# Two encoder layers on one core: the borders of the stages laid out anew, and the first stage ordered by hand

## The chip, the cores and the metric

The kernel runs on one core of one Trainium2 chip. The time is device microseconds of one execution; lower is better. A core has TensorE (PE, matmuls; its weight loads are listed as PEld), VectorE (DVE), ScalarE (ACT), GpSimd (POOL) and SyncE (SP, which here issues every DMA). SBUF is the working memory, PSUM the eight banks that matmuls write. Each engine takes its instructions in a fixed order, the one in which the program was laid out.

## The reference, cut to what matters

512 tokens of width 1024 pass through two layers. `c` gives six rows (shift, scale, gate, twice) per layer.

```
c_act = silu(c)
for l in range(2):
    mod = c_act @ w_mod[l] + b_mod[l]
    sh1, sc1, gt1, sh2, sc2, gt2 = split(mod, 6)
    h = rms_norm(x, g_norm_mix[l]) * (1 + sc1) + sh1
    q_d, k_d, v_d, cq, ckv, k_rope = split(h @ w_in[l])
    o_dil = dilated_attention(rms_norm(q_d), rms_norm(k_d), v_d, positions)   # 8 heads of 64
    o_mla = latent_attention(cq, ckv, k_rope, positions, ...)                 # 8 heads, low-rank q and kv, rotary part
    x = x + gt1 * (concat[o_dil, o_mla] @ w_out[l])
    h = rms_norm(x, g_norm_mlp[l]) * (1 + sc2) + sh2
    x = x + gt2 * (square(relu(h @ w_mlp_in[l])) @ w_mlp_out[l])
```

## The kernel before

x is kept transposed: eight tiles `xT[j]` of 128 features by 512 tokens. Every matmul operand is split into a high and a low part, and each product is three matmuls (`mm3`, L237: lines L238, L239, L240): high by high, low by high, high by low. A weight tile is loaded into a `raw` buffer by a DMA, its high part made by ACT (L233) and its low part by POOL (L234), into buffers named `wh` and `wl`, four each (`load_split`, L229).

The order of work on each engine is not the program's. A planner simulates the program with estimated costs and gives each engine its next ready instruction, the earliest in the program first; that order is then fixed. Three things bind it: `tc.manual_schedule(engines=...)` keeps the instructions of a block on the named engines in the program's order among themselves, `keep_in_program_order` pins one instruction behind what its engine has been given before, and `issue_after` queues what follows on an engine behind one instruction. Buffers are shared by tag: a tile waits until one of the tag's buffers is free (`BUFS`, L61). PSUM has four banks `mm`, two `sc` and two `tr`.

The stages, layer by layer:

- **Setup (L86 to L154, L188 to L196).** Load c, x and small tables; silu of c, spread over the 128 partitions by two matmuls with a matrix of ones (L117) and copied to the SBUF tile `cb` (L118); the squares of x are summed (L121 to L128); the angles of the rotary part are made on POOL and their sines on ACT (L133 to L151), with one load of ACT's function table before and one after.
- **First stage of layer 0 (L694 to L753).** Sixteen rows of w_mod (512 KB each) are loaded and multiplied with `cb` on DVE, which also sums them (`mod_block`, L162). From the sum over x comes 1/rms (`inv_rms`, L244). For each k of eight feature groups: u = x/rms on DVE, high part of h and the full value on ACT (L732, L733), low part alternately on POOL (L735) and DVE (L723), then matmuls with two groups of weights: PR0 (columns of the first pair of dilated heads: q, k, v, 384 columns) and W (the latent columns: cq, ckv and the rotary key, 416 columns), for all four blocks of 128 tokens, which takes all eight PSUM banks. Only DVE is ordered by hand here. After the last k come the chains: the norms of q and k (`chain`, L428; `rsqrt_tiny`, L218), the same for W (L504), the transposes (`tail`, L453 and L521), the rotary tables (`rope_tables`, L484) and the distances for the bias (`distances`, L304).
- **First stage of layer 1 (L755 to L759).** The same weights, PR0 for the four token blocks, then W; norms of the two token halves come from the end of the MLP before (L883).
- **Attention (L761 to L788).** Eight stages of two heads, `st` 0 to 3 dilated, 4 to 7 latent. While the heads of one stage run, `weave` puts in the projection of the next (PR1, PR2, ...), weight loads, the remaining rows of w_mod and, from stage 4, the output projection of the dilated half (`out_dil`). The due times are the numbers of `TUNE`. A head (L327) takes four query blocks: scores, softmax, four transposes into a `tr` bank (L358), the high and low part of the transposed weights (L361, L362), and at the end the product with the values (L368) and the output (L371, L641, L642).
- **Projection 2 (L790 to L812).** The output projection of the latent half, for each half of 256 tokens: eight output tiles, each a sum over four head pairs; the fourth needs the last stage's output. In the first half up to three tiles have their first three products made before a fourth product is asked for. Then `norm` (L277) for that half.
- **MLP (L839 to L883).** Groups of 8, 8, 8, 4 and 4 blocks of 128 hidden features, each with its part of the second matrix. The first four blocks run by token halves, all others over 512 tokens. In layer 0 two rows of w_mod are taken at each other block (`next_mod`, L855).

Of the kernel before, what the change touches and what calls it, by code (L numbers as in the profile page):

```python
# [16 lines left out]
L = 2  # L17
# [20 lines left out]
    MV5=(6.55,), MP0=(3.45,), MP1=(8.6,), W0=(13.54,), W1=(21.5,), W2=(33,),  # L38
# [4 lines left out]
def trunk(ctx: ExitStack, tc: tile.TileContext, a):  # L43
# [28 lines left out]

    def ps(tag, shape=(128, 512)):
        return psum.tile(list(shape), F32, tag=tag, bufs=BUFS[tag], name=nm(tag))
# [15 lines left out]
    cols = [col(N_COL, f"cols{l}") for l in range(L)]  # L90
    SY.dma_start(cols[0], a["cols"][0])
    posc = const.tile([128, 4], I32, name="posc")
    SY.dma_start(posc, a["pos"].rearrange("(t p) -> p t", p=128))
    inv = col(16, "inv")
    SY.dma_start(inv, bass.AP(tensor=a["inv"].tensor, offset=a["inv"].offset, ap=[[0, 128], [1, 16]]))

    xT = [const.tile([128, S], F32, name=f"x{j}") for j in range(8)]
    for j in range(8):
        SY.dma_start(xT[j], a["xT"][j])
    ones = const.tile([128, 128], F32, name="ones")  # L100
# [3 lines left out]


# [5 lines left out]
    cb = const.tile([128, D], F32, name="cb")  # L111
    for i in range(2):
        p = ps("sc", (128, 4, 128))
        dg = s2([128, 4, 128])
        for k in range(4):
            V.tensor_scalar(dg[:, k], ident, cs[:, 4 * i + k:4 * i + k + 1], None, op0=OP.mult)
        T.matmul(p.rearrange("p k c -> p (k c)"), ones, dg.rearrange("p k c -> p (k c)"), start=True, stop=True)  # L117
        A.activation(cb[:, 512 * i:512 * i + 512], p.rearrange("p k c -> p (k c)"), AF.Copy)  # L118


    sq0 = s2(tag="o")  # L121
    for j in range(8):
        if j == 0:
            A.activation(sq0, xT[j], AF.Square)
        else:
            sq = s2(tag="P")
            A.activation(sq, xT[j], AF.Square)
            V.tensor_tensor(sq0, sq0, sq, op=OP.add)  # L128


    pf = col(4, "pf")
    V.tensor_copy(pf, posc)
    ang, kf, w_ = s2([128, 4, 16]), s2([128, 4, 16]), s2([128, 4, 16], tag="b")  # L133
    for t in range(4):
        G.tensor_scalar(ang[:, t], inv, pf[:, t:t + 1], 0.0, op0=OP.mult, op1=OP.add)
    G.tensor_scalar(kf, ang, 1.0 / (2 * math.pi), 12582912.0, op0=OP.mult, op1=OP.add)
    G.tensor_scalar(kf, kf, -12582912.0, 0.0, op0=OP.add, op1=OP.add)
    c1 = 6.28125
    c2 = float(np.float32(np.round((2 * math.pi - c1) * 2.0 ** 20) / 2.0 ** 20))
    c3 = 2 * math.pi - c1 - c2  # L140
    for cc in (c1, c2, c3):
        G.tensor_scalar(w_, kf, -cc, 0.0, op0=OP.mult, op1=OP.add)
        G.tensor_tensor(ang, ang, w_, op=OP.add)
    PI_ = 3.1415925
    G.tensor_scalar(ang, ang, PI_, -PI_, op0=OP.min, op1=OP.max)
    A.activation(kf, ang, AF.Abs)
    G.tensor_scalar(kf, kf, -1.0, math.pi / 2, op0=OP.mult, op1=OP.add)
    sin = const.tile([128, 4, 16], F32, name="sin")
    cos = const.tile([128, 4, 16], F32, name="cos")
    A.activation(sin, ang, AF.Sin)  # L150
    A.activation(cos, kf, AF.Sin)  # L151
    pre = A.preload_act_table_set("natural_log_exp_and_others")
    tc.keep_in_program_order(pre)
    ctx.enter_context(tc.issue_after(pre.ins))  # L154
# [7 lines left out]
    def mod_block(l, i, tag="raw", pool_=False, pin=False, out=None):  # L162
        out = modc[l][:, i:i + 1] if out is None else out
        w = t4(tag, [128, D], F32)
        SY.dma_start(w, a["wmod"][l, i])
        if pool_:
            G.tensor_tensor(w, w, cb, op=OP.mult)  # L167
            A.activation(w, w, AF.Copy, accum_out=out)
        else:
            r = V.scalar_tensor_tensor(w, w, 1.0, cb, op0=OP.mult, op1=OP.mult, accum_out=out)  # L170
            if pin:
                tc.keep_in_program_order(r)
# [19 lines left out]
    def first_norm(j):  # L192

        A.activation(modc[0][:, j:j + 1], mraw[:, j:j + 1], AF.Identity, bias=cols[0][:, C_BMOD + j:C_BMOD + j + 1])
        A.activation(amix[0][:, j:j + 1], mraw[:, 8 + j:9 + j], AF.Identity, bias=gb0[:, j:j + 1],
                     scale=cols[0][:, C_GMIX + j:C_GMIX + j + 1])  # L196

# [31 lines left out]
    def load_split(src, n, raw="raw"):  # L229
        raw = t4(raw, [128, 1024], F32)[:, :n]  # L230
        hi, lo = t4("wh", [128, 1024])[:, :n], t4("wl", [128, 1024])[:, :n]
        SY.dma_start(raw, src)
        A.activation(hi, raw, AF.Copy)  # L233
        G.tensor_tensor(lo, raw, f(hi), op=OP.subtract)  # L234
        return hi, lo
# [8 lines left out]
    def inv_rms(p, v, y, t):  # L244

        V.tensor_scalar(v, p, 1.0 / D, EPS, op0=OP.mult, op1=OP.add)
        A.activation(t, v, AF.Ln)
# [3 lines left out]
        V.scalar_tensor_tensor(y, t, 1.5, p, op0=OP.add, op1=OP.mult)  # L251
# [52 lines left out]
    def distances():  # L304

        posr = s2([128, S], I32)
        SY.dma_start(posr, bass.AP(tensor=a["pos"].tensor, offset=a["pos"].offset, ap=[[0, 128], [1, S]]))
# [10 lines left out]
        dist = [t4("ot", [128, 2, S], F32) for _ in range(2)]  # L318
        for qb in range(4):
# [3 lines left out]
        g = t4("ot", [128, 896], F32)  # L323
        SY.dma_start(g, a["lnc"])
        return dist, g
# [52 lines left out]
    for l in range(L):  # L378
# [19 lines left out]
        def group(src, n):  # L398
            ws = {}

            def load(i, raw="raw"):
                hi, lo = load_split(src[i], 2 * n, raw)
                ws[i] = (hi.rearrange("p (k n) -> p k n", k=2), lo.rearrange("p (k n) -> p k n", k=2))

# [4 lines left out]
            return [lambda i=i, **kw: load(i, **kw) for i in range(4)], step  # L409

        def blocks(w, n, step, chain):
            for tb in range(4):
                st = {}

                def mm(k, tb=tb, st=st):
                    if k == 0:
                        st["b"] = ps("mm")
# [5 lines left out]
        def dil_prep(pr, k_outer=False):  # L423
            w = dict(mm=[], chain=[])
            w["load"], step = group(a["win"][l, pr], 384)
            R = {}

            def chain(tb, bank):  # L428
# [4 lines left out]
                if t == 0:  # L433
                    R[half] = t4("pt" if k_outer else "zz", [128, 2, 4, 2, 64], F32)
                    R["sq"], R["bank"] = s2([128, 8, 64]), bank
                sq = R["sq"]
                A.activation(sq[:, 4 * t:4 * t + 4].rearrange("p h d -> p (h d)"), bank[:, 0:256], AF.Square, scale=1.0 / 8)
                src = bank[:, 256:384].rearrange("p (h d) -> p h d", h=2)
                vt = R["VD"][:, tb]
                A.activation(vt[:, :, 0], src, AF.Copy)  # L440
                V.tensor_tensor(vt[:, :, 1], src, f(vt[:, :, 0]), op=OP.subtract)
                if t == 0:
                    return

                v = small(8)
                V.tensor_reduce(v, sq, axis=AX.X, op=OP.add)
                rs = rsqrt_tiny(v, 8, bank)
                for u, bk in enumerate((R["bank"], bank)):
                    src = bk[:, 0:256].rearrange("p (h o d) -> p h o d", h=4, o=1).to_broadcast([128, 4, 2, 64])
# [496 lines left out]
```

## Time and profile before

| | |
|---|---|
| median of 3 runs | 1368.05 us (1367.66 to 1368.26) |
| the profiled execution | 1368.62 us |
| its span in the profile | 1366.8 us |
| mean granted clock of TensorE | 0.975 |
| bytes moved | 167.59 MB |
| rows of w_mod multiplied in the MLP of layer 0 (L170, `pt`) | 56, 1804 ns each |

The profile is of one execution. Its rows count an engine's busy time; idle time before an instruction is put down to what released it. A row of the table by stretch gives start and end, the length, the busy time of each engine with its number of instructions, the mean clock that was granted to TensorE, the share of the DMA engines that were busy, and GB/s. A row of the timeline gives the start, the length, the engine, the line, the operation, the tiles and, in brackets, the idle time before it and what ended it.

### The profile page before, as it was taken

How to read it: one execution, taken by the hardware profiler on the slowest of the kernel's cores; microseconds unless marked ns; L12 is line 12 of the kernel's file. 1: busy time of each engine (PE TensorE's matmuls, PEld its weight loads, DVE VectorE, ACT ScalarE, POOL GpSimd, SP SyncE). 2: the span in 40 equal slices, each digit the busy share in tenths (PEclk: the TensorE clock that was granted, in tenths of full speed). 3: DMA queues.
4: the chain of work that ended last, by engine and by line, in shares of the span. 5: the costliest groups of instructions: out<-in, count | busy, mean ns of one | idle time of the engine just before them, and what ended most of it. 6: DMA issues, size and time to landing. Idle time of an engine off the chain costs nothing.

```text
span 1366.8 us, 19167 instructions
## 1 busy us (share of the span) xinstructions
PE 1275.1 (93%) x6922; PEld 1109.2 (81%) x6922; DVE 752.4 (55%) x1588; ACT 673.9 (49%) x1389; POOL 651.0 (48%) x504
## 2 busy tenths in 40 slices
PE   3879979898899999999998999999889999999999
PEld 2878867787888888888898988788688888888888
DVE  6677888876661752825574566987662122121223
ACT  5567888875532332322344766887654133232321
POOL 5636785571554444444443533454145444444441
PEclk7989999999999999999999999999999999999999
DMA  9325552331163663845522433211013223223321
GB/s 344 111 95 170 181 164 90 118 124 63 63 224 115 218 229 103 294 142 188 170 82 63 132 124 111 74 45 62 1 63 108 93 93 108 93 93 100 101 93 62
DMA packets 57247, 167.59 MB, mean 123 GB/s; under 512 B 8641, under 2 KB 10817, under 8 KB 57153
## 3 DMA queue, kind: packets, MB, share of 16 engines
q1 hardware_dynamic: 57152, 166.38, 37.0%
q8 instruction: 54, 0.88, 0.3%
q14 instruction: 41, 0.33, 0.1%
HBM read 155.87 MB, written 10.49 MB: 122 GB/s over the span
## 4 chain that ended last, share of the span: by engine, by line
PE 72%; DVE 6%; ACT 5%; issue 4%; POOL 4%; DMA 3%; POOLq 0%; DVEq 0%; ACTq 0%
PE mm L238 21%; PE mm L239 21%; PE mm L240 21%; PE tr L368 3%; PE tr L358 2%; POOL wl L234 2%; DMA raw<-in_wout_dram 1%; DVE pt L362 1%; ACT wh L233 1%; DVE P L343 1%; POOL raw L167 1%; PE sc L238 1%; PE mm L459 1%; PE sc L239 1%; PE sc L240 1%
## 5 line engine op out<-in xcount | busy, mean ns | idle before, releaser
L234 POOL TENSOR_TENSOR wl<-raw,wh 128x1024 fp32r<-128x1024 f32 (+3 forms) x188 | 425.4, 2266 | 449.6 <-ACT wh L233 431.4
L233 ACT ACTIVATE wh<-raw 128x1024 fp32r<-128x1024 f32 (+3 forms) x188 | 189.0, 1005 | 273.7 <-PE mm L240 206.4
L649 DVE SCALAR_TENSOR_TENSOR x<-mm,mod,x 128x512 f32<-128x512 f32 (+1 forms) x144 | 89.1, 629 | 259.9 <-PE mm L240 259.5
L238 PE MATMUL mm<-h,wh 128*128 128x512 f32 (+1 forms) x608 | 224.5, 370 | 7.1 <-ACT h L274 7.1
L239 PE MATMUL mm<-h,wl 128*128 128x512 f32 (+1 forms) x608 | 224.6, 370 | 0.0
L240 PE MATMUL mm<-h,wh 128*128 128x512 f32 (+1 forms) x608 | 221.7, 369 | 1.1 <-POOL h L271 1.1
L238 PE MATMUL mm<-ot,wh 128*128 128x512 f32 (+1 forms) x448 | 154.1, 347 | 4.9 <-ACT ot L641 4.1
L239 PE MATMUL mm<-ot,wl 128*128 128x512 f32 (+1 forms) x448 | 153.1, 344 | 0.0
L240 PE MATMUL mm<-ot,wh 128*128 128x512 f32 (+1 forms) x448 | 150.7, 346 | 0.6 <-POOL ot L642 0.6
L822 ACT ACTIVATE P<-mm 128x512 f32<-128x512 f32 (+1 forms) x72 | 39.2, 551 | 203.9 <-PE mm L240 203.9
L238 PEld LDWEIGHTS mm<-h,wh 128*128 128x128 f32 x608 | 116.2, 191 | 26.1 <-ACT h L274 7.5
L239 PEld LDWEIGHTS mm<-h,wl 128*128 128x128 f32 x608 | 116.1, 191 | 19.0 <-POOL wl L234 0.3
L240 PEld LDWEIGHTS mm<-h,wh 128*128 128x128 f32 x608 | 114.5, 190 | 20.3 <-POOL h L271 1.6
L823 DVE SCALAR_TENSOR_TENSOR mm<-mm,P 128x512 f32<-128x512 f32 (+1 forms) x72 | 45.4, 636 | 138.6 <-ACT P L822 138.6
L238 PE MATMUL mm<-wh,h 128*128 128x384 f32 (+1 forms) x288 | 98.7, 357 | 15.8 <-ACT h L732 9.8
L239 PE MATMUL mm<-wh,h 128*128 128x384 f32 (+1 forms) x288 | 101.8, 354 | 5.1 <-POOL h L735 3.6
L238 PE MATMUL mm<-qk,wh 128*128 128x512 f32 (+1 forms) x288 | 105.3, 366 | 1.0 <-DVE x L649 1.0
L239 PE MATMUL mm<-qk,wl 128*128 128x512 f32 (+1 forms) x288 | 105.2, 365 | 0.0
L240 PE MATMUL mm<-qk,wh 128*128 128x512 f32 (+1 forms) x288 | 105.2, 365 | 0.0
L355 POOL TENSOR_SCALAR P<-P,hs 128x512 f32<-128x512 f32 x64 | 48.4, 756 | 116.5 <-DVE hs L348 94.8
L240 PE MATMUL mm<-wl,h 128*128 128x384 f32 (+1 forms) x288 | 100.2, 351 | 0.0
L170 DVE SCALAR_TENSOR_TENSOR pt<-pt,cb 128x1024 f32<-128x1024 f32 x56 | 99.1, 1804 | 0.0
(248 smaller groups left out, 2667.1 us busy)
## 6 DMA issues: line engine op xcount, KB each, us to landing
raw<-in_w_dram SPq DMA_DIRECT2D x64, 512.0 KB, 3.3
pt<-in_wmod_dram SPq DMA_DIRECT2D x56, 512.0 KB, 4.8
raw<-in_w2a_dram SPq DMA_DIRECT2D x48, 512.0 KB, 3.4
raw<-in_wmod_dram SPq DMA_DIRECT2D x24, 512.0 KB, 3.6
raw<-in_win_dram SPq DMA_DIRECT2D x30, 384.0 KB, 3.2
bias<-b SPq DMA_DIRECT2D x32, 256.0 KB, 2.1
raw<-in_wout_dram SPq DMA_DIRECT2D x16, 512.0 KB, 3.4
raw<-in_w2b_dram SPq DMA_DIRECT2D x16, 512.0 KB, 3.3
```

Of the source, the lines that this page charges most:

```text
L170: r = V.scalar_tensor_tensor(w, w, 1.0, cb, op0=OP.mult, op1=OP.mult, accum_out=out)
L233: A.activation(hi, raw, AF.Copy)
L234: G.tensor_tensor(lo, raw, f(hi), op=OP.subtract)
L238: T.matmul(out, sh, mh, start=first, stop=False)
L239: T.matmul(out, sl, mh, start=False, stop=False)
L240: T.matmul(out, sh, ml, start=False, stop=last)
L355: G.tensor_scalar(P, P, r_, 0.0, op0=OP.mult, op1=OP.add)
L358: T.transpose(tr[:, kc], P[:, kc * 128:(kc + 1) * 128], ident)
L368: T.matmul(po[:, HALF[qh]], vals(hd, kc), pt[qh][w][:, kc], start=(kc == 0 and w == 0), stop=(kc == 3 and w == 1))
L649: V.scalar_tensor_tensor(xT[j][:, hf], p, gt[:, j:j + 1], xT[j][:, hf], op0=OP.mult, op1=OP.add)
L822: A.activation(r, p, AF.Relu)
L823: V.scalar_tensor_tensor(p, p, 0.0, r, op0=OP.max, op1=OP.mult)
```

## The change

It has six parts; the lines are of the diff below.

1. **silu's row in PSUM.** The two `tr` banks become one tile `trp`, used in turns by every later user of the tag. In the first stage it holds silu's row (`cbp`), which DVE reads directly; the copy to `cb` is made at the stage's end.
2. **The first stage by hand.** SP, DVE, ACT and POOL are all in the program's order. x is loaded before the small tables. The exponential's table is loaded at the start; the sines move to the end of the stage (`rotary`, on DVE), with the two table loads behind them. Two of the squares go to POOL; 1/rms goes to PSUM; every low part of h goes to POOL. The rows of w_mod are loaded ahead into `qk` buffers, weights are loaded and split at fixed places. In the loop over k only PR0's four token blocks and W's first are multiplied; W's other blocks come after the loop, the second in an `sc` bank, the third and fourth in `mm` banks that PR0's chain sets free. The distances are made at the end of the loop; the rotary tables move to stage 1.
3. **Projection 2.** In the first half, tiles 4 to 7 get their first three products and a first addition to x, tiles 0 to 3 get them and are held in their banks; the fourth products come last. The second half stays as it was. The last weight tile of it is split into `zz` buffers.
4. **The MLP's first eight blocks** run by token halves (four before). Their weight tiles are split into `pt`, `qk` and `wh`/`wl` buffers. In layer 0 the eight rows of w_mod of that group come during the second half.
5. **Layer 1's first stage**: PR0 blocks 0 and 1, W blocks 0 and 1, then PR0 2 and 3, W 2 and 3. W's weights are loaded at once, into `ot` and `pt` buffers; PR0's blocks 2 and 3 use `sc` banks; PR0's norms are made for each block instead of for each pair.
6. `TUNE`: W1 from 21.5 to 29.5.

```diff
+    trp = psum.tile([128, 2, 512], F32, name="trp")
+    turn = [0]
     def ps(tag, shape=(128, 512)):
+        if tag == "tr":
+            turn[0] ^= 1
+            v = trp[:, turn[0]]
+            return v.rearrange("p (a b) -> p a b", a=shape[1]) if len(shape) == 3 else v
...
+    def exp_tables():
+        pre = A.preload_act_table_set("natural_log_exp_and_others")
+        tc.keep_in_program_order(pre)
+        ctx.enter_context(tc.issue_after(pre.ins))
...
-        A.activation(cb[:, 512 * i:512 * i + 512], p.rearrange("p k c -> p (k c)"), AF.Copy)
...
+    def rotary():
...
+        A.activation(sines, sines, AF.Sin)
+        exp_tables()
...
-    def inv_rms(p, v, y, t):
+    def inv_rms(p, v, t):
+        A.activation(t, p, AF.Ln, bias=epsc, scale=1.0 / D)
         V.tensor_scalar(v, p, 1.0 / D, EPS, op0=OP.mult, op1=OP.add)
-        A.activation(t, v, AF.Ln)
...
+            with tc.manual_schedule(engines={E.SP, E.DVE, E.Activation, E.Pool}):
+                for k in range(8):
+                    mods(k)
+                    if k % 2 == 0:
+                        weights(k // 2)
...
+                A.activation(sqp, xT[0], AF.Square)
+                for j in range(1, 8):
+                    sq = s2(tag="P")
+                    if j in (1, 4):
+                        G.tensor_tensor(sq, xT[j], xT[j], op=OP.mult)
+                    else:
+                        A.activation(sq, xT[j], AF.Square)
+                    V.tensor_tensor(sq0 if j == 7 else sqp, sqp, sq, op=OP.add)
+                T.matmul(p, ones, sq0, start=True, stop=True)
...
+                splits(0)
+                mod_mul(8)
+                mod_mul(0)
+                inv_rms(p, v, t)
+                for k in range(8):
...
+                    V.tensor_tensor(u, xT[k], p, op=OP.mult)
+                    first_norm(k)
+                    A.activation(hi, u, AF.Identity, bias=be, scale=ga)
+                    A.activation(u, u, AF.Identity, bias=be, scale=ga)
+                    G.tensor_tensor(lo, u, f(hi), op=OP.subtract)
+                    if k % 2 == 0 and k < 6:
+                        splits(k // 2 + 1)
+                    if k < 7:
+                        mod_mul(9 + k)
+                        mod_mul(k + 1)
+                    for tb in range(4):
+                        PR[0]["step"](banks[tb][:, :384], k, tb)
+                    W["step"](lbanks[0][:, :W_C], k, 0)
+                gains()
+                dist = distances(posr)
+                for i in range(2):
+                    A.activation(cb[:, 512 * i:512 * i + 512], cbp[:, 512 * i:512 * i + 512], AF.Copy)
+            lbanks.append(ps("sc"))
+            for k in range(8):
+                W["step"](lbanks[1][:, :W_C], k, 1)
...
+            for fn in PR[1]["load"][:2]:
+                fn(keep=True)
             for tb in range(4):
                 PR[0]["do_chain"](tb, banks[tb])
+            for tb in (2, 3):
+                lbanks.append(ps("mm"))
+                for k in range(8):
+                    W["step"](lbanks[tb][:, :W_C], k, tb)
...
+            for n, (w, tb) in enumerate(((PR[0], 0), (PR[0], 1), (W, 0), (W, 1), (PR[0], 2), (PR[0], 3), (W, 2), (W, 3))):
+                ev += spread(w["mm"][tb], 4 * n, 4 * n + 3.6) + [(4 * n + 3.8, w["chain"][tb])]
...
+            if l == 0 and st == 1:
+                ev += [(2, W["rope"])]
...
+        hf, held = HALF[0], {}
+        for j in (4, 5, 6, 7, 0, 1, 2, 3):
+            p = ps("mm")[:, :256]
+            out_lat(j, p, hf, (0, 1, 2), True, j >= 4)
+            if j >= 4:
+                add_x(j, hf, p, gt1)
+            else:
+                held[j] = p
+        for j in range(8):
+            p = held[j] if j < 4 else ps("mm")[:, :256]
+            out_lat(j, p, hf, (3,), j >= 4, True)
+            add_x(j, hf, p, gt1)
+        norm(hf, amlp[l], modc[l][:, 24:32], h2h, h2l)
...
+            tags = ("wh", "wl") if i >= 4 else ("pt", "pt") if i < 2 else ("qk", "qk")
...
+            ws = [w1_tile(i) for i in range(8)] if grp[0] == 0 else []
...
                 for hf in HALF:
-                    for i in range(4):
+                    for i in range(8):
                         mlp1(i, hf, ws[i])
+                        if l == 0 and hf.start and i:
+                            next_mod(tag="pt", pin=True)
+                            if i == 7:
+                                next_mod(tag="pt", pin=True)
```

More of the change, by code (lines that the diff above doesn't have):

```diff
@@ L99, in trunk @@
         SY.dma_start(xT[j], a["xT"][j])
+    cols = [col(N_COL, f"cols{l}") for l in range(L)]
+    SY.dma_start(cols[0], a["cols"][0])
     ones = const.tile([128, 128], F32, name="ones")
@@ L146, in trunk @@
[L146 to L154, printed above, removed]
+        T.matmul(cbp[:, 512 * i:512 * i + 512], ones, dg.rearrange("p k c -> p (k c)"), start=True, stop=True)
@@ L407, in step, with blocks @@
                     ws[k // 2][0][:, k % 2], ws[k // 2][1][:, k % 2], k == 0, k == 7)
-            return [lambda i=i, **kw: load(i, **kw) for i in range(4)], step
-        def blocks(w, n, step, chain):
+            return [lambda i=i, **kw: load(i, **kw) for i in range(4)], step, put
+        def blocks(w, n, step, chain, tags=("mm",) * 4):
             for tb in range(4):
@@ L424, in dil_prep @@
             w = dict(mm=[], chain=[])
-            w["load"], step = group(a["win"][l, pr], 384)
+            w["load"], step, w["put"] = group(a["win"][l, pr], 384)
             R = {}
@@ L441, in chain @@
[L441 to L449, printed above, removed]
-                    scl = rs[:, 4 * u:4 * u + 4].rearrange("p (h o d) -> p h o d", o=1, d=1).to_broadcast([128, 4, 2, 64])
-                    V.tensor_tensor(R[half][:, u], src, scl, op=OP.mult)
+                    R[half] = t4("pt" if pr == 0 else "zz", [128, 2, 4, 2, 64], F32)
@@ new lines, in chain @@
+                if nb == 2:
+                    values()
+                if len(got) == nb:
+                    v = small(4 * nb)
+                    V.tensor_reduce(v, sq, axis=AX.X, op=OP.add)
+                    rs = rsqrt_tiny(v, 4 * nb, bank)
+                    for u, (t_, bk) in enumerate(got):
+                        src = bk[:, 0:256].rearrange("p (h o d) -> p h o d", h=4, o=1).to_broadcast([128, 4, 2, 64])
+                        scl = rs[:, 4 * u:4 * u + 4].rearrange("p (h o d) -> p h o d", o=1, d=1).to_broadcast([128, 4, 2, 64])
+                        V.tensor_tensor(R[half][:, t_], src, scl, op=OP.mult)
@@ L479, in dil_prep @@
             else:
-                blocks(w, 384, step, chain)
+                blocks(w, 384, step, chain, ("mm", "mm", "sc", "sc") if pr == 0 else ("mm",) * 4)
             return w
@@ L501, in latent @@
             w = dict(mm=[], chain=[])
-            w["load"], step = group(a["winc"][l], W_C)
+            w["load"], step, w["put"] = group(a["winc"][l], W_C)
             def chain(tb, bank):
@@ L741, in trunk, with mods, weights, splits @@
-            gains()
+            ml, wr = {}, {}
+            def mods(k):
+                ml[8 + k] = mod_load(0, 8 + k, "qk")
+                ml[k] = mod_load(0, k, "qk")
+            def weights(i):
+                raw = ("raw", "zz")[i % 2]
+                wr[i] = load(a["win"][0, 0, i], 768, raw), load(a["winc"][0, i], 2 * W_C, raw)
+            def splits(i):
+                PR[0]["put"](i, *split(wr[i][0], 768))
+                W["put"](i, *split(wr[i][1], 2 * W_C, ("ot", "ot") if i < 2 else ("wh", "wl")))
@@ L745, in trunk @@
+            for fn in PR[0]["tail"]:
                 fn()
```

234 lines of the change are left out of this document (106 added, 128 removed).

## The prediction

> **What bounds the kernel now.** I read the page's head first, then the busy time by stretch of the span, then the waits of TensorE (PE), and last the timeline at each border.
>
> ```profile
> span 1366.8 us, 19167 instructions
> PE 1275.1 (93%) x6922; PEld 1109.2 (81%) x6922; DVE 752.4 (55%) x1588; ACT 673.9 (49%) x1389; POOL 651.0 (48%) x504
> ```
>
> PE is the bound: 1275.1 of 1366.8 us, so 91.7 us of idle time is all that an edit without fewer matmuls can win, plus what the matmuls lose at a low granted clock. The table by stretch says where the idle time lies (first number: length; second: PE busy; PEclk is the mean granted clock).
>
> ```profile
> core 0: us, PE busy (x) PEld busy (x) DVE busy (x) ACT busy (x) POOL busy (x), PEclk, DMA share, GB/s
> 0.00:25.50 25.50, 5.86 (x6) 1.68 (x6) 14.70 (x43) 14.26 (x24) 11.62 (x20) 0.74 0.89 323
> 45.00:70.30 25.30, 21.78 (x104) 19.63 (x102) 14.57 (x27) 14.73 (x30) 18.25 (x18) 0.93 0.13 35
> 70.30:80.30 10.00, 4.94 (x21) 3.88 (x22) 8.62 (x25) 7.52 (x35) 3.30 (x2) 0.83 0.42 139
> 116.00:315.00 199.00, 180.10 (x1115) 157.59 (x1113) 159.47 (x387) 158.23 (x371) 133.03 (x137) 0.97 0.41 132
> 315.00:332.00 17.00, 12.80 (x88) 10.82 (x88) 9.21 (x19) 10.07 (x21) 4.65 (x5) 1.00 0.23 79
> 350.40:376.00 25.60, 21.49 (x161) 20.87 (x161) 15.85 (x42) 14.15 (x34) 13.57 (x19) 0.93 0.17 55
> 709.60:735.00 25.40, 20.78 (x105) 19.09 (x104) 15.71 (x40) 14.32 (x32) 15.84 (x20) 0.87 0.25 71
> 965.00:987.00 22.00, 16.88 (x116) 14.29 (x115) 12.78 (x26) 14.74 (x31) 4.74 (x6) 1.00 0.01 1
> 1005.60:1031.00 25.40, 21.30 (x160) 20.69 (x159) 16.04 (x42) 13.86 (x33) 13.66 (x18) 0.93 0.16 57
> ```
>
> Length less busy time: 19.6 + 3.5 + 5.1 us in the first stage's rows, 4.2 and 5.1 at the two last heads (315 and 965), 4.1 and 4.1 where the MLP begins (350 and 1005), 4.6 where layer 1 begins (709). The waits give the names:
>
> ```profile
> PE mm L238 <- ACT h L274: 11.1, 3, 4.1
> PE mm L238 <- ACT h L732: 9.8, 2, 9.5
> PE mm L238 <- ACT ot L641: 4.1, 2, 2.1
> PE mm L459 <- ACT mm L223: 3.0, 1, 3.0
> ```
>
> The 11.1 us are three waits for the first h of the second token half (two MLPs, one layer start); 9.8 is the first h of the program; 4.1 is the last head's output, once per layer; 3.0 the first chain. The change puts other matmuls in front of each of these.
>
> **First stage, the start.** Before, it runs so:
>
> ```profile
> 13.98 2.08 PE L713 MATMUL sc<-o,ones 128*128 128x512 f32 x2 [5.41 <-DVE o L128]
> 15.60 1.28 ACT L150 ACT_TABLE_LOAD   x1
> 19.82 0.61 ACT L247 ACTIVATE b<-b 128x512 f32<-128x512 f32 x1
> 21.79 0.69 DVE L249 TENSOR_TENSOR b<-b,sc 128x512 f32<-128x512 f32 x1 [4.81 <-ACT sc L248]
> 23.95 0.69 DVE L728 TENSOR_TENSOR pt<-x,P 128x512 f32<-128x512 f32 x1
> 25.55 1.65 PE L238 MATMUL mm<-wh,h 128*128 128x384 f32 x4 [9.48 <-ACT h L732]
> ```
>
> The sum of squares is ready at 16.06, but the logarithm (L247) starts at 19.82, behind the sine table, the second load and a split. The change moves sines and both loads out, drops two copies of silu's row, gives two squares to POOL and issues x before three small transfers. I put the sum at 13.9 (about 2 us earlier, an estimate); the logarithm now stands, by hand, behind two splits that wait for the first weights, so about 14.5. From 19.82 to 25.55 was 5.7 us, of which steps of 0.61 to 0.69 us in series make nearly all; they stay, one of them taken ahead. The first matmul comes at about 19.5: 6 us gained, bounds 3 (splits late) and 7.
>
> The change has DVE read PSUM in some thirty of these operations. In the rows an operation with one operand in PSUM (L249) took 0.69 us, one with both in SBUF (L728) 0.69: I take no difference. [...]
>
> **First stage, the pace.**
>
> ```profile
> 15.00:20.00 5.00, 1.06 (x2) 0.00 (x0) 1.98 (x5) 4.62 (x9) 1.29 (x3) 0.50 1.03 412
> qk<-in_wmod_dram SPq DMA_DIRECT2D x8, 512.0 KB, 9.5
> 25.16 1.22 DVE L170 SCALAR_TENSOR_TENSOR qk<-qk,cb 128x1024 f32<-128x1024 f32 x1
> 30.37 3.01 DVE L170 SCALAR_TENSOR_TENSOR qk<-qk,cb 128x1024 f32<-128x1024 f32 x1
> 39.04 0.34 PE L239 MATMUL mm<-wh,h 128*128 128x384 f32 x1
> 43.39 0.33 PE L239 MATMUL mm<-wh,h 128*128 128x384 f32 x1
> ```
>
> The DMA engines are full at 412 GB/s. Nothing of the bytes goes: 16 rows of 512 KB, eight weight tiles, x, some 13.7 MB, 33 us; begun near 4.5, the last row lands near 38 (an estimate from this rate). That stays a bound. What goes is the delay behind it: a product with silu's row takes 1.22 us alone, but 3.01 where it meets POOL with two SBUF operands; with the row in PSUM I take 1.22 for all, bounds 1.22 and 3.01 for each of 16. DVE's share per k is then 2 x 1.22 and one 0.7 multiplication, 3.1 us; eight of them from 18.5 end near 41 to 43, and the last h at 45 to 46. One k costs PE 4.35 us now (39.04 to 43.39, 12 matmuls of 384 columns and 12 of 416); split by columns that is 2.1 for PR0 and 2.25 for W, 0.19 a matmul; with one token block of W instead of four, 2.1 + 0.6 = 2.7. The k loop ends at about 47.5.
>
> ```profile
> 65.79 1.28 POOL L735 TENSOR_TENSOR h<-pt,h 128x512 fp32r<-128x512 f32 x1
> 67.78 0.39 ACT L437 ACTIVATE s<-mm 128x256 f32<-128x256 f32 x1 [5.76 <-PE mm L240]
> 72.47 1.28 DVE L451 TENSOR_TENSOR pt<-mm,st 128x512 f32<-128x512 f32 x2
> 80.33 0.48 PE L238 MATMUL mm<-wh,h 128*128 128x384 f32 x1
> 62.85 0.32 POOL L491 TENSOR_TENSOR rot<-cos,gr 128x64 f32<-128x64 f32 x1
> ```
>
> Before, the last low part of h was made only at 65.79, long after those bytes, and PE met the next projection (PR1) at 80.33 with the chain exposed in between. After, W's other three token blocks (24 x 0.19 us = 4.5 each) lie beside that chain. Block 1 can start when its bank is free (about 41) and ends near 51. Blocks 2 and 3 wait for PR0's first two banks. The new wait is here: the chain's ACT steps are queued behind the sines and two table loads (1.28 us each), which wait for a dozen short DVE steps: about 47. DVE's distance steps stand there too. From 67.78 to 73.7 the first half of the chain took 6 us, so the banks come at 53; PE is idle for about 2 us, runs 9 us of W, some of it at a low clock, and meets PR1 at 64: 16 us earlier than 80.33. Given back: two of PR1's four weight tiles need buffers that W holds until 64, 3 us; and fourteen rotary steps of POOL (0.32 us each, 4.5 in all) now stand in stage 1's queue, ahead of bias and split work there: 3 us. Net 10; ends 4 and 18.
>
> **Projection 2, by half and early (both layers).** Before the last output arrives PE can now do 8 x 9 matmuls instead of 3 x 9 for the first half. At 256 columns one takes 0.12 us:
>
> ```profile
> 355.74 0.28 PE L240 MATMUL mm<-h,wh 128*128 128x256 f32 x1
> ...
> 357.42 0.28 PE L239 MATMUL mm<-h,wl 128*128 128x256 f32 x1
> 399.75 0.39 PE L240 MATMUL mm<-h,wh 128*128 128x512 f32 x1
> ...
> 401.79 0.39 PE L240 MATMUL mm<-h,wh 128*128 128x512 f32 x1
> ```
>
> (14 steps in 1.68 us, and 9 of 512 columns in 2.04: 0.227.) That is 5.4 us more filler for idle time of 4.2 and 5.1. All four banks are then held for the last output: what does not fit before it waits. Later, only 24 matmuls stand between it and the half's norm instead of 69, and the second half's 96 (11.5 us) cover that norm. Four more x updates on DVE lie beside PE. The first MLP tiles' splits, now in other buffers, may be laid ahead of the last output on ACT and POOL. I take 2.5 per layer; ends 0 and 4.5.
>
> **The MLP's first 8 blocks by halves (both layers).** Cost: 4 more blocks x 24 x (0.240 - 0.227) = 1.3 us per layer. Gain: 8 x 24 x 0.12 = 23 us of first-half matmuls from 350.4 on reach 373; the second half's h came 11.5 us of four blocks and 0.6 + 3.5 us of waits after 350.4, at 366; the row's 4.1 idle go and up to 1.8 of low clock (0.07 x 25.6). 4.1 + 1.5 - 1.3 = 4.3 at best; the norm now shares DVE, ACT and POOL with four more blocks and earlier splits, so 2.5 per layer; ends -1.3 (lost) and 4.5. For the halving the trace's rows give 1.3 us. [...]
>
> **Layer 1's start.** PR0's and W's first two token blocks (8.4 + 9 us) now stand ahead of the second half: 4.6 idle and up to 3.3 of low clock (0.13 x 25.4). W's four splits must be on time on POOL, whose queue also carries the norm. I take 4; ends 0 and 6.
>
> **Sum.** 10 + 5 + 5 + 4 = 24 us. The profiled execution took 1368.62 us, 1.8 around its span; the median of the three runs is 0.57 lower, so 1368.05 - 24 = **1344**.
>
> **Rivals.** (1) *The start's gain comes back in the heads.* Row 116:315 has PE at 180 of 199 us with DVE and ACT at 159 and 158: if these set the heads' pace, and POOL's rotary steps with them, the 10 us go: 1354. For it: all three near full. Against: PE is the fullest. (2) *The gaps close fully*: 18 + 9 + 5 + 4 = 36: 1332. Against: each border has its own new queue. (3) *The edits miss*: the planner lays PE's order out by its estimates, early products land outside the gaps, the start stays with the transfers: about 1367, no change. For it: the old early products, 27 matmuls, left the 2.1 us wait for the last output as well. (4) *Slower.* The two transpose banks become one tile used in fixed turns.
>
> ```profile
> 321.34 0.60 PE L358 MATMUL tr<-ident,P 128*128 128x128 f32 x4
> 323.66 0.60 ACT L361 ACTIVATE pt<-tr 128x512 fp32r<-128x512 f32 x1 [0.17 <-PE tr L358]
> 322.85 0.69 DVE L362 TENSOR_TENSOR pt<-tr,pt 128x512 fp32r<-128x512 f32 x1
> ```
>
> If waits are kept for the whole tile, transposes, copy and subtraction (1.9 us) run in series for each of 128 query blocks, where now two overlap. It decides from 0.19 us exposed per block (24 / 128); at 0.4 it costs 51: 1395. Against: other tiles are written and read in slices at the same time.
>
> **Numbers.** Forecast 0.58, rival 1 0.20, rival 2 0.10, rival 3 0.05, rival 4 0.07. Faster by over 0.2% (2.7 us, about what a measurement tells apart) is the forecast with rivals 1 and 2: 0.88; same 0.05; slower 0.07. The range 1331 to 1360 takes in the forecast with the bounds of its terms, most of rival 1 and half of rival 2.
>
> **What would show it.** First projection matmul near 19.5, PR1 near 64, products with silu's row at 1.22 throughout; no wait of PE for L274's successor over 1 us; waits for the last output below 1 us; the MLP's second half starting at once. Wrong: the first stage's end later than 75; transposes waiting for L362's successor far longer than now; a new long wait of PE for a split at a border.

## The result, and the profile after

The changed kernel takes 1515.85 us (median of 4 runs, 1514.28 to 1517.97) against 1367.94 for the kernel before (median of 4, 1367.66 to 1368.26): 1.1075 times as long, 95% interval 1.105 to 1.11, 148 us slower. The prediction was 1344. Line numbers of "after" below are those of the changed kernel: L252 to L254 for the three matmuls of a product, L369 the transposes of a query block, L372 and L373 their copy and subtraction, L379 the product with the values, L381 and L382 the two steps of a head's output.

The head of the page of after:

```profile
span 1512.5 us, 19697 instructions
PE 1335.1 (88%) x7114; PEld 1154.5 (76%) x7114; DVE 756.5 (50%) x1652; ACT 689.9 (46%) x1417; POOL 638.2 (42%) x496
```

The span grew by 145.7 us. PE's idle time grew from 91.7 to 177.4, which is 85.7 of it. The other 60.0 are in PE's busy time. It has 7114 matmuls, 192 more than before, since some are cut into halves; but E4 below has the same 7114 and is busy for 1272.2 us, so the time comes from matmuls that ran slower, at a mean granted clock of 0.939 and not 0.975 (0.98 in E4). The waits of PE in after (total, times, longest):

```profile
PE sc L252 <- ACT P L358: 45.2, 37, 3.3
PE trp L369 <- DVE o L382: 33.8, 19, 4.1
PE sc L495 <- DVE hs L354: 24.2, 25, 2.5
PE trp L369 <- DVE pt L373: 9.3, 8, 1.5
PE mm L252 <- DVE pt L472: 7.3, 1, 7.3
PE mm L252 <- ACT h L777: 6.7, 1, 6.7
```

The first four kinds, in the same order, in before:

```profile
PE sc L238 <- ACT P L347: 0.9, 3, 0.3
PE tr L358 <- DVE o L371: 5.2, 7, 1.2
PE sc L472 <- DVE hs L343: 12.1, 12, 1.8
PE tr L358 <- DVE pt L362: 1.8, 3, 0.8
```

These four are inside the heads: scores wait for the softmax of an earlier block, and transposes (L369, tile `trp`) wait for a head's output or a subtraction. The last two of after belong to the first stage. The waits for the first h of a second half are gone (11.1 us in three before; one of 0.4 for L289 now). A timeline of after, all engines but the weight loads and DMAs, late in layer 0:

```profile
390.89 2.17 PE L379 MATMUL trp<-pt,qk 128*128 128x256 f32 x16 [1.41 <-DVE pt L373]
...
391.23 0.69 POOL L366 TENSOR_SCALAR P<-P,hs 128x512 f32<-128x512 f32 x1
394.68 1.06 ACT L234 ACTIVATE wh<-raw 128x1024 fp32r<-128x1024 f32 x1 [3.90 <-DMA raw<-in_w_dram]
395.76 0.59 ACT L381 ACTIVATE o<-trp 64x512 f32<-64x512 f32 x1
...
396.39 0.68 DVE L382 TENSOR_TENSOR o<-trp,o 64x512 f32<-64x512 f32 x1 [4.82 <-ACT o L381]
397.13 1.12 PE L369 MATMUL trp<-ident,P 128*128 128x128 f32 x4 [4.06 <-DVE o L382]
```

The weights P of the next block are ready at 391.92 (L366). Its transposes go to the other bank: a head takes five turns, so the next head begins with the bank that the output did not use. They still start at 397.13, when L382 has read the output, and that one was late because ACT stood behind a weight split that waited for its DMA. The same holds for the whole trace: of the heads' 512 transposes, 98 start in before while DVE runs a subtraction (L362) or an output (L371); in after none does.

The next table gives the start of the head's last step (L371 before, its successor elsewhere) by heads, in us; the kernels E3 to E13 are explained below.

| head | before | after | E3 | E4 | E5 | E9 | E13 |
|---|---|---|---|---|---|---|---|
| layer 0, 1st | 116.1 | 109.5 | 113.3 | 105.7 | 115.9 | 115.9 | 105.1 |
| 2nd | 133.4 | 138.3 | 128.2 | 120.7 | 133.1 | 133.1 | 119.9 |
| 4th | 168.7 | 179.6 | 175.1 | 169.0 | 168.3 | 168.2 | 168.1 |
| 13th | 305.5 | 357.0 | 318.1 | 304.8 | 304.0 | 303.9 | 304.7 |
| 16th | 328.9 | 412.5 | 348.9 | 338.6 | 335.1 | 327.4 | 327.9 |
| layer 1, 1st | 784.4 | 857.6 | 794.4 | 784.3 | 779.7 | 779.0 | 779.6 |
| 8th | 892.4 | 987.3 | 889.7 | 879.5 | 876.9 | 873.4 | 873.8 |
| 16th | 984.3 | 1135.7 | 989.3 | 976.7 | 975.6 | 965.7 | 966.1 |
| span | 1366.8 | 1512.5 | 1365.9 | 1355.1 | 1353.3 | 1349.0 | 1349.6 |

After is 6.6 us ahead at its first head and loses 90 between the first and the last head of layer 0, and 78 between those of layer 1. Between the layers and behind the last head it is faster than before by 10 and 5.7.

### The profile page after: what moved, and what is told of

Its sections match the earlier page's. It is cut to its first block, busy times and chain, and to the rows that moved or that the text cites. A ratio compares the mean times of both kernels' runs of the same rounds, so it can differ in the third digit from the quotient of the medians.

```text
span 1512.5 us, 19697 instructions
## 1 busy us (share of the span) xinstructions
PE 1335.1 (88%) x7114; PEld 1154.5 (76%) x7114; DVE 756.5 (50%) x1652; ACT 689.9 (46%) x1417; POOL 638.2 (42%) x496
## 4 chain that ended last, share of the span: by engine, by line
PE 71%; DVE 9%; ACT 7%; DMA 4%; issue 4%; POOL 4%; SPq 0%; DVEq 0%; POOLq 0%; ACTq 0%
PE mm L254 19%; PE mm L252 19%; PE mm L253 19%; PE trp L379 4%; PE trp L369 3%; PE sc L252 2%; POOL wl L235 1%; ACT P L358 1%; ACT pt L372 1%; DVE P L354 1%; PE sc L253 1%; DVE qk L741 1%; PE sc L254 1%; DMA raw<-in_wmod_dram 1%; PE sc L495 1%
## 5 line engine op out<-in xcount | busy, mean ns | idle before, releaser
L235 POOL TENSOR_TENSOR wl<-raw,wh 128x1024 fp32r<-128x1024 f32 (+2 forms) x173 | 391.6, 2266 | 464.6 <-ACT wh L234 460.0
L234 ACT ACTIVATE wh<-raw 128x1024 fp32r<-128x1024 f32 (+2 forms) x173 | 173.8, 1005 | 291.2 <-PE mm L254 214.8
L252 PE MATMUL mm<-h,wh 128*128 128x512 f32 (+1 forms) x544 | 198.8, 365 | 1.4 <-ACT h L666 1.1
L253 PE MATMUL mm<-h,wl 128*128 128x512 f32 (+1 forms) x544 | 198.4, 365 | 0.0
L254 PE MATMUL mm<-h,wh 128*128 128x512 f32 (+1 forms) x544 | 198.3, 365 | 0.0
L252 PE MATMUL mm<-ot,wh 128*128 128x512 f32 (+1 forms) x416 | 150.4, 363 | 9.2 <-ACT ot L666 6.3
L254 PE MATMUL mm<-ot,wh 128*128 128x512 f32 (+1 forms) x416 | 145.3, 357 | 1.2 <-POOL ot L667 1.2
L373 DVE TENSOR_TENSOR pt<-trp,pt 128x512 fp32r<-128x512 f32 x128 | 88.1, 688 | 93.4 <-ACT pt L372 92.9
L369 PE MATMUL trp<-ident,P 128*128 128x128 f32 x512 | 90.3, 305 | 43.4 <-DVE o L382 33.8
L369 PEld LDWEIGHTS trp<-ident,P 128*128 128x128 f32 x512 | 68.5, 157 | 66.3 <-issue 29.0
L372 ACT ACTIVATE pt<-trp 128x512 fp32r<-128x512 f32 x128 | 76.4, 597 | 92.3 <-PE trp L369 88.9
L252 PEld LDWEIGHTS mm<-h,wh 128*128 128x128 f32 x544 | 102.8, 189 | 18.6 <-ACT h L666 1.6
L254 PEld LDWEIGHTS mm<-h,wh 128*128 128x128 f32 x544 | 103.0, 190 | 16.2
L253 PEld LDWEIGHTS mm<-h,wl 128*128 128x128 f32 x544 | 102.8, 189 | 16.2
L366 POOL TENSOR_SCALAR P<-P,hs 128x512 f32<-128x512 f32 x64 | 45.9, 717 | 148.2 <-DVE hs L359 135.9
L252 PE MATMUL mm<-qk,wh 128*128 128x512 f32 (+1 forms) x288 | 105.3, 366 | 1.0 <-DVE x L674 1.0
L254 PE MATMUL mm<-qk,wh 128*128 128x512 f32 (+1 forms) x288 | 105.2, 365 | 0.0
```

The costliest lines, as they stand in the source:

```text
L234: ra = A.activation(hi, raw, AF.Copy)
L235: rg = G.tensor_tensor(lo, raw, f(hi), op=OP.subtract)
L252: T.matmul(out, sh, mh, start=first, stop=False)
L253: T.matmul(out, sl, mh, start=False, stop=False)
L254: T.matmul(out, sh, ml, start=False, stop=last)
L366: G.tensor_scalar(P, P, r_, 0.0, op0=OP.mult, op1=OP.add)
```

## The experiments

**The tile.** Theory: waits are kept for the whole tile `trp` (rival 4 of the prediction). Rivals: the fixed turns themselves; another part of the change that spoils the heads. Four kernels tell them apart. Each ratio here and below is to runs of before on the same chip, whose medians lay from 1368.7 to 1372.6.

E1, the kernel before with the tile alone:

```
     def ps(tag, shape=(128, 512)):
+        if tag == "tr":
+            turn[0] ^= 1
+            v = trp[:, turn[0]]
...
```

> The kernel before with nothing changed but the two transpose banks: one tile of two banks, used in fixed turns. One-tile theory (waits are kept for the whole tile, so a block's transposes, its copy, its subtraction and a head's last output run in series): the loss of 148 us and the 20 to 24 us that the other parts should bring add up here, 1368 + 148 to 172 = 1516 to 1540. Fixed-turns theory (the bank that comes next by turn is the busy one): the same number. Other-parts theory (the first stage by hand, the halves or the new order make the heads slow): no change, 1368 within 5.

Measured: 1545.69 us (1542.15 to 1549.23, 2 runs), 1.1286 times before (1.1255 to 1.1316). Its waits of PE:

```profile
PE sc L245 <- ACT P L354: 50.3, 41, 1.4
PE sc L479 <- DVE hs L350: 29.1, 28, 2.2
PE trp L365 <- DVE o L378: 25.5, 17, 2.8
```

The same three waits as in after, from this edit alone, and again none of the 512 transposes starts during a subtraction or an output. It costs 176 us, 1.38 for each of 128 query blocks, more than the 148 to 172 that I had expected.

E2, the changed kernel with two tiles of one bank, in the same fixed turns; the row is copied to `cb` at the start:

```
-    trp = psum.tile([128, 2, 512], F32, name="trp")
+    trs = [psum.tile([128, 512], F32, name=f"trp{i}") for i in range(2)]
...
-            v = trp[:, turn[0]]
+            v = trs[turn[0]]
```

> The changed kernel, with two tiles of one bank each in the same fixed turns; silu's row is copied to SBUF before the first stage's products read it. One-tile theory: waits are now kept for each bank, the loss goes, and the time is that of the prediction's sum, 1344 to 1360. Fixed-turns theory: the turns are as they were, so 1500 to 1516. Other-parts theory: 1510 to 1520.

E3, the same with the `tr` tag as before (a bank is released and taken anew):

> The changed kernel with the two transpose banks as in the kernel before (released and taken anew for each use), silu's row in SBUF. One-tile theory: as with two tiles, 1344 to 1360. Fixed-turns theory: 1344 to 1360 too. Other-parts theory: 1510 to 1520.

E4, as E3, but with the row in PSUM during the first stage, in a pool of its own that is closed there:

```
+    first = ExitStack()
+    trp = first.enter_context(tc.tile_pool(name="first", bufs=1, space=bass.MemoryType.PSUM)).tile(...)
...
+            first.close()
+            later.append(ctx.enter_context(tc.tile_pool(name="later", bufs=1, space=bass.MemoryType.PSUM)))
```

> The changed kernel, silu's row in PSUM in the first stage as the change has it, but its two banks are given back after the first stage and are then taken anew for each use. One-tile and fixed-turns theories: 1344 to 1360, within 3 us of the version with the row in SBUF, since the product took as long from PSUM as from SBUF. Other-parts theory: 1510 to 1520.

Measured: E2 1370.18 (1.0007 times before, 0.9998 to 1.0016), E3 1369.15 (1.000, 0.999 to 1.001), E4 1356.61 (0.9901, 0.9884 to 0.9917). E2 has the turns of the changed kernel and none of its loss, so the turns are not the cause; two banks in one tile are. In E2, 88 of the 512 transposes start while a subtraction or an output runs. The theory stands. But only E4 lies within the 1344 to 1360 that I expected of all three: E2 and E3 gain nothing over before. E3 and E4 differ by 12.5 us where I expected 3 at most. What differs between them is the place of silu's row and when it is copied to `cb`. The view of the line that multiplies with it gives least, median and longest time in ns, then the start of the first and of the last product in us, in E3 (row in SBUF) and in E4 (row in PSUM):

```profile
L735 DVE SCALAR_TENSOR_TENSOR qk<-qk,cb x16: 1207/1908/2977, 13.9 to 49.8; 128x1024 f32<-128x1024 f32 x16
```

```profile
L740 DVE SCALAR_TENSOR_TENSOR qk<-qk,trp x16: 1205/1216/1222, 12.9 to 42.0; 128x1024 f32<-128x1024 f32 x16
```

The 16 products take 30.7 us together in E3 and 19.4 in E4. In E3 each one that took over 1.6 us ran beside a POOL instruction for more than 1.1 us of its time; in E4 such neighbours lengthened none. With the row in PSUM the last product starts 7.8 us earlier; my expectation for E4 compared undisturbed products only. The remaining 5 us or so of the 12.5 appear later, among the heads, and no run says what they come from. In before the 16 products take 23.7 us, so against before the row's new place saves only 4.3 us of DVE: most of the loss that it avoids (7.0 of 11.3 us) came with the new stage, which gives every low part of h to POOL.

**Where the rest of the 24 went.** E4 is 13 us faster than before, not 24. E5 has the borders alone (parts 3 to 6 of the change); first stage, row and banks are those of before.

> The kernel before with the borders changed alone: projection 2 early, the first 8 blocks of MLP by halves, layer 1's start in its new order; the first stage, its row and the transpose banks are those of before. Theory: in the version with released banks the stretch from layer 0's last head to the end took 21 us less than before, while layer 0 up to there took 10 us more, so the borders alone bring 19 to 22 and this takes 1347 to 1351, less than the 1356.6 with the new first stage. Rival (the first stage brought its 10 us and the borders brought little): 1362 to 1368. Between them: the parts do not add up.

Measured: 1355.36 (0.9901, 0.9886 to 0.9916). The borders bring 13.5, not 21, which lies between theory and rival, and the new first stage on top of them nothing (E4). I had read gains off two traces as if they added up.

E6 moves distances (with the load of the positions that they read), sines and the copies of the row behind PR0's transposes. E7 puts rope's steps back behind W's transposes; its edit:

```
-            if l == 0 and st == 1:
-                ev += [(2, W["rope"])]
...
             W["tail"]()
+            W["rope"]()
```

> The version with released banks, but the distances of the positions, the sines with their two table loads and the copy of silu's row come behind pair 0's chain and transposes and no longer ahead of them. Theory (pair 0's chain starts 10 us late behind them, its banks come free at 63.5 and not at 53, and W's last blocks and pair 1's products are late by that): the wait of 7.3 us ahead of W's third block goes, pair 1's products start at 70 to 75, and the time falls by 6 to 10 from 1356.6, to 1347 to 1351. Rival (what is late is the bias of the first heads, which needs the distances): 1355 to 1362.

> The version with released banks, with rope's 14 steps on POOL of layer 0 behind W's transposes as in the kernel before, and not in stage 1. Theory (these steps are what stretches the time between the second and the third head's output from 17 us to 26): the time falls by 6 to 9, to 1347 to 1351. Rival (the stretch comes from the order of loads and of pair 1's products): 1354 to 1359, the stretch stays at 24 to 27.

Measured: E6 1362.73 (0.9955, 0.994 to 0.997), E7 1356.23 (0.9905, 0.9889 to 0.9922). E7: the 14 POOL steps cost nothing that can be told apart; the second and third output lie 26.1 us apart in both E4 and E7, as the rival had it. E6 is a miss of another kind: no longer ordered by hand, the sines moved ahead, into the k loop. The timeline of ACT in E6, and of PE:

```profile
43.50 1.28 ACT L151 ACT_TABLE_LOAD   x1
48.83 0.31 ACT L151 ACTIVATE sines<-sines 128x128 f32<-128x128 f32 x1 [4.04 <-DVE sines L150]
```

```profile
51.31 0.69 PE L251 MATMUL mm<-wh,h 128*128 128x384 f32 x1 [6.30 <-ACT h L774]
```

E8 therefore writes PR0's chain into the hand-made order, ahead of the distances:

```
                 gains()
+                for tb in range(4):
+                    PR[0]["do_chain"](tb, banks[tb])
                 dist = distances(posr)
```

> The version with released banks; pair 0's chain is written into the hand-ordered first stage, ahead of the distances, the sines with their two table loads and the copies of silu's row, which the late-distances version did not hold back (its sines moved up into the k loop instead, and their table load kept ACT from the rows of h for 6.3 us). Theory (the chain's place behind them is what makes W's third block wait 7.3 us): the chain starts at 47 to 48 and not at 57, the wait goes, pair 1's products start at 72 to 76 and not at 81.6, and the time is 1348 to 1352. Rival (what is gained at the start comes back in the heads, whose order is set by other waits): first head 5 us or more earlier, but the last head of layer 0 within 3 of 338.6, and 1354 to 1358.

Measured: 1363.47 (0.9954, 0.9938 to 0.9969), slower than E4, and my theory was wrong. The wait of W's third block fell from 7.3 us to 0.54, but PE then waited twice for what had been moved back. PE in E8, at W's third block, PR0's transposes and W's transposes:

```profile
57.52 0.43 PE L251 MATMUL mm<-ot,h 128*128 128x416 f32 x1 [0.54 <-DVE pt L471]
```

```profile
72.67 0.90 PE L481 MATMUL mm<-ident,pt 128*128 128x128 f32 x3 [4.97 <-DVE qk L490]
```

```profile
79.79 0.66 PE L549 MATMUL mm<-ident,zz 128*128 128x128 f32 x2 [5.15 <-DVE zz L536]
```

PR1's products began at 92.75 and not at 81.62. Distances, sines, table loads and copies are about 10 us of one series on DVE and ACT (61.4 to 71.4 in E8). Ahead of PR0's chain (E4) PE waits for it, and behind that chain (E8) too; E6 did not test a third place, since its sines slipped.

E9 is the kernel before with layer 1's start alone (part 5 with TUNE); E10 adds projection 2 to that (E5 without the halves of the MLP):

> The kernel before with layer 1's start alone: pair 0's and W's blocks by turns, their weights in other buffers, the chain one block at a time. From the traces of before and of the version with all borders: there the first head of layer 1 came 4.7 us earlier and its last one 8.7 us earlier, with nothing gained up to the end of layer 0's MLP. Theory (the start of layer 1 brings those 8.7): 1358 to 1362. The prediction's term of 4: 1364 to 1366. Rival (it comes from the planner's new order elsewhere): 1367 to 1370.

> The version with the borders alone, without the halves of MLP's first 8 blocks (4 blocks by halves, 4 whole, as in the kernel before). Prediction's term for the halves: 2.5 in each layer, so 5 slower than that version, 1359 to 1361. Rival (the cost of the smaller products eats the gain): 1354 to 1357.

Measured: E9 1351.33 (0.9872, 0.9851 to 0.9894), E10 1352.65 (0.9881, 0.9858 to 0.9905). Layer 1's start brings 18 us, more than I expected of it and more than the whole of E5; E10 too is faster than theory and rival had it. From E9 over E10 to E5 the medians rise by 1.3 and 2.7; each step is within the intervals, the 4.0 together at their edge. In no case did projection 2 or the halves win. The heads of the pages of E9 and E5:

```profile
span 1349.0 us, 19204 instructions
PE 1269.4 (94%) x6922; PEld 1106.8 (82%) x6922; DVE 754.2 (56%) x1620; ACT 675.7 (50%) x1405; POOL 650.2 (48%) x504
```

```profile
span 1353.3 us, 19637 instructions
PE 1273.6 (94%) x7114; PEld 1118.0 (83%) x7114; DVE 762.5 (56%) x1644; ACT 679.6 (50%) x1421; POOL 651.9 (48%) x504
```

E5 has 4.2 us more busy time, and its idle time is 79.7 us against 79.6. What was idle at the borders was idle elsewhere: in layer 1 the time from the 13th to the 16th output is 23.6 us in E9 and 30.0 in E5, and 27.0 in E10, which has projection 2's new order alone. Around the last head, PE in E9 and E5:

```profile
967.10 0.38 PE L249 MATMUL mm<-ot,wh 128*128 128x256 f32 x1 [2.06 <-ACT ot L666]
```

```profile
977.25 0.39 PE L249 MATMUL mm<-ot,wh 128*128 128x256 f32 x1 [2.29 <-ACT ot L666]
...
981.00 0.58 PE L251 MATMUL mm<-ot,wh 128*128 128x256 f32 x1 [1.87 <-POOL ot L667]
```

The early products stood among the last heads: between the 13th and the 16th output of layer 1 PE starts 48 matmuls of projection 2 in E5 and in E10, and 12 in E9. The wait for the last output was no shorter for that (2.06 in before as well).

E11 takes from E9 the chain of one block at a time (`nb = 2` in layer 1 too); E12 gives that chain to pairs 1 to 3 of layer 0 as well (`nb = 2 if k_outer else 1`).

> The version with layer 1's start alone, but the chain of a dilated pair's projections takes two blocks at a time in layer 1 too, as in the kernel before; the new order and the other buffers stay. That version was 18 us faster than before, of which 5 lay at layer 1's first head and 13 between the second and the eighth. Theory A (the chain one block at a time brings the 13, since the next pair's banks come free earlier): 1362 to 1366. Theory B (the new order and buffers bring all of it): 1350 to 1354.

> The version with layer 1's start alone, and the chain one block at a time in layer 0 too (for pairs 1 to 3; pair 0 of the first stage stays). Theory A: layer 0's heads gain what layer 1's gained between the second and the eighth, up to 13, so 1338 to 1348. Theory B: no gain, 1349 to 1356. If it is the fastest, it is the version to keep.

Measured: E11 1358.44 (0.9931, 0.991 to 0.9952), E12 1360.78 (0.9931, 0.9905 to 0.9958). So of the 18 us about 10 are the order and the buffers, 7 the one-block chain, between theories A and B. One kind of PE's waits from 800 to 920 us (total, times, longest), in before, E11 and E9:

```profile
PE sc L472 <- DVE hs L343: 8.3, 7, 1.8
```

```profile
PE sc L495 <- DVE hs L354: 5.7, 5, 1.8
```

```profile
PE sc L495 <- DVE hs L354: 0.2, 1, 0.2
```

The scores' bank waits for DVE's maximum. I read it so that with a chain of one block less stands ahead of that maximum on DVE; the order on DVE itself was not shown. In layer 0 (E12) the same edit made the kernel slower, which neither theory had: by 9 us against E9, with intervals that do not overlap, and the last head of layer 0 comes at 339.0 us and not at 327.4. Why is not settled.

E13 is the new first stage with released banks and layer 1's start, without projection 2 and the halves. E14 moves in it the sines to the start: positions loaded behind two rows of x, `rotary()` ahead of the squares, the Sin behind their sum.

> The new first stage with released banks and layer 1's start, without projection 2's new order and without the halves of MLP (both cost time in the versions before). If the parts add up: 1356.6 less the 4.0 by which the version with layer 1's start alone beat the one with all borders, so 1351 to 1354; the new first stage is then worth nothing against the old one. If the first stage has a gain that the other parts hid: 1341 to 1349.

> The same, with the sines computed ahead of the first products: the positions come in behind two rows of x, the 14 small steps run on DVE ahead of the sums of squares, the Sin with its two table loads runs on ACT in the 2.95 us in which it waited for the first weights. Theory (sines and tables behind the k loop hold pair 0's chain, and by it W's third block and pair 1): the chain starts at 51 to 53 and not at 57, W's third block at 57 to 60 and not at 63.65, layer 0's later heads move by as much, and the time is 3 to 6 below the version without this. Rival (pair 1's chain and the weights behind the stores of the bias set the heads): within 2 of it, or above.

Measured: E13 1352.36 (0.9844, 0.9817 to 0.9871), E14 1355.87 (0.9876, 0.9845 to 0.9906). E13 and E9 cannot be told apart; both beat before by 1.3 to 1.6%. In E14 the wait ahead of W's third block fell only from the 6.46 us of E13 to 5.04, since distances, copies and a weight split still stood before the chain, which began at 56.61 (56.92 in E13); and the first matmul of the k loop came at 24.44 and not at 21.63. It is not faster.

## Why the prediction was wrong, point by point

**The step that failed: the sum of 24 us has no term for the merged tile.** The forecast put the loss of overlap between two query blocks at nothing. Rival 4 was the case, and both its chance and its price were wrong. The prediction named the mechanism and what would show it (transposes waiting far longer for L362's successor; the waits for a head's output, which cost more, it did not name), gave it 0.07 and, at "0.4" a block, 1395. Measured are 1.38 us a block for the tile alone (E1, 176 us) and 1.24 in the change (1515.85 less E4's 1356.61, by 128: 159 us). The series of 1.9 us was in the text; taking a fifth of it as exposed had no row behind it, and the rows quoted there, two blocks overlapping, should have said that the overlap was needed. "Other tiles are written and read in slices at the same time" did not carry over to this tile; why not, no run settles.

The other terms of the sum were off as well, by far less. Their own ends, added up, also reach further (1326 to 1367) than the stated 1331 to 1360.

**The first stage: 10 predicted, about 0 measured** (E13 against E9, E4 against E5). The steps, in after:

```profile
22.44 1.01 PE L252 MATMUL mm<-wh,h 128*128 128x384 f32 x2 [6.71 <-ACT h L777]
```

```profile
45.69 1.28 ACT L152 ACT_TABLE_LOAD   x1
50.69 0.31 ACT L152 ACTIVATE sines<-sines 128x128 f32<-128x128 f32 x1 [3.72 <-DVE sines L151]
51.02 1.28 ACT L110 ACT_TABLE_LOAD   x1
52.31 2.57 ACT L334 ACTIVATE ot<-pt,pc 128x512 f32<-128x512 f32 x4
54.78 1.06 ACT L791 ACTIVATE cb<-trp 128x512 f32<-128x512 f32 x2
55.74 0.38 ACT L454 ACTIVATE s<-mm 128x256 f32<-128x256 f32 x1
```

```profile
62.43 0.68 PE L252 MATMUL mm<-ot,h 128*128 128x416 f32 x1 [7.27 <-DVE pt L472]
```

```profile
79.72 0.42 PE L252 MATMUL mm<-wh,h 128*128 128x384 f32 x1
```

- The first matmul: 22.44, not 19.5 (25.55 before): 3.1 us of 6, the lower bound that the text gave.
- The products with silu's row: 1.203 to 1.223 us throughout. Right, and most of what E4 has over E3, the same stage with the row in SBUF. Undisturbed, the product took as long from PSUM as from SBUF: least times of 1205 ns (E4) and 1207 (E3).
- The k loop: PR0's last product ended at 52.88, not at 47.5; PE had W's second block ahead of it from 45.8 on.
- The chain's start: "about 47", measured 55.74. This is where the first stage's term failed. The text named the sines, the two table loads and DVE's distance steps, but gave them no time of their own behind the k loop: DVE's steps ahead of the Sin kept ACT for 3.72 us, and the four distance activations (2.57) and the two copies (1.06) were not in the text at all.
- The banks: 62.43, not 53; W's last two blocks then 11 us more; PR1 at 79.72, not 64 (80.33 before). Of "16 us earlier" 0.6 was left. The first head still comes 10 us earlier in E4, but by the fourth the lead is gone (169.0 against 168.7). That is rival 1's outcome. Of the causes named there, rope's steps cost nothing (E7); the pace of DVE and ACT was not tested.

**Projection 2 and the MLP's halves: 10 predicted, about 4 lost**, at the edge of the intervals. The waits for h did go, as said, but the sum took idle time at a border for time won. The planner laid the early products among the last heads, which took longer for it, and the wait for the last output stayed (2.29 us in E5, 2.06 in before): the prediction's rival 3 had seen this. Idle time as a whole did not fall (79.7 us in E5, 79.6 in E9). The halving costs about 4.2 us of PE's busy time for 192 halved matmuls, where the rows had given 2.6.

**Layer 1's start: 4 predicted, 18 measured.** By the first head 5 us are won (784.4 to 779.0). The rest came in the heads behind it, about 7 from the one-block chain (E11) and the remainder from the new order and buffers, none of which the text weighed.

**The sum.** Before 1368; the tile +159 on top of E4; layer 1's start −18; projection 2 and halves +4; first stage about 0: 1513 against 1515.85. The 159 was itself taken from 1515.85, so what this sum tests is the other three terms: 1354 against E4's 1356.61.

## What to carry to other kernels

In this kernel two buffers that are to overlap had to be two tiles, or be released and taken anew (the merged tile alone cost 176 us in E1; E2 and E3, without it, took as long as before); ask of every merged tile who reads one part while another is written, and price it by the whole series until a run shows less (here 1.38 us a block, of 1.9). An idle gap on a nearly full engine is not yet a gain (PE's idle time was 79.7 us in E5, with projection 2 and the halves, and 79.6 in E9, without them): look at what the work that fills it covered at its old place. A step that is moved "to the end" stands ahead of whatever is next on each of its queues (in after PR0's chain began at 55.74 us and not at about 47); list all its instructions there, and time them from rows.

## What was unexpected of the hardware

The loss shows twice: in the heads of after PE had more idle time, and it was granted less clock there, at which the matmuls took longer. Two stretches of after late in layer 0's heads (length, PE's busy time; the third number from the end is the granted clock):

```profile
300.00:340.00 40.00, 26.88 (x128) 21.39 (x128) 17.98 (x35) 21.63 (x39) 17.95 (x11) 0.83 0.33 106
340.00:400.00 60.00, 38.70 (x189) 31.29 (x188) 22.95 (x49) 25.61 (x52) 13.33 (x12) 0.75 0.10 31
```

From the first head of layer 0 to its last the mean is 0.86 in after (109.5 to 412.5 us), and 0.97 in before (116.1 to 328.9). E1 has exactly the matmuls of before, so the head of its page shows the size:

```profile
span 1547.5 us, 19229 instructions
PE 1354.5 (88%) x6922; PEld 1158.9 (75%) x6922; DVE 751.9 (49%) x1588; ACT 683.7 (44%) x1389; POOL 640.0 (41%) x504
```

Of 180.7 us of longer span, 79.4 are the same 6922 matmuls being busy for longer, at a mean granted clock of 0.919 (0.975 before). The clock accounts for nearly all of that: 1275.1 us times 0.975 / 0.919 is 1353. The other 101.3 us are idle time, so the span grew by 1.8 times what the idle time grew by. It came without a long gap: from 300 to 400 us, inside layer 0's heads, no gap of PE in E1 is longer than 1.47 us, PE is busy for 68% of the time, and the granted clock is 0.69 in the first 40 us and 0.70 in the last 60. Before has one gap of 3.53 us in these 100 us (other work from 329 us on), is busy for 89%, and keeps 0.96 and 0.97. What sets the granted clock, no run shows.
